# A fourth buffer for the low halves of the streamed weights, and two 16 KB pairs for the large activations

## The chip, the cores and the metric

The kernel runs on one core of a Trainium2 chip. The metric is the device time of one execution in microseconds (us); lower is better. The core's engines work side by side, each through its own list of instructions: TensorE (PE) multiplies, with its weight loads shown apart as PEld; VectorE (DVE) and ScalarE (ACT) do the elementwise work; GpSimd (POOL) does next to nothing here; SyncE (SP) issues the DMA transfers. Instructions wait for each other by semaphores.

## The reference

A sequence of 256 tokens of width 1024 goes through two blocks of two layers each, all in float32.

```python
# block 1, for l in range(2)
sh1, sc1, gt1, sh2, sc2, gt2 = split(silu(c) @ w_ada[l] + b_ada[l], 6)
u = x * (1 + sc1) + sh1
y = mixer(u, ...)          # proj = u @ w_in; attention (8 heads, rope) and a conformer conv, 31 taps
x = layer_norm(ALPHA * x + (1 + gt1) * y, ...)
u = x * (1 + sc2) + sh2
h = square(relu(u @ w_up[l])) @ w_down[l]
x = layer_norm(ALPHA * x + (1 + gt2) * h, ...)
# block 2, two layers: rmsnorm, a mixer of three attention branches (dilated windows, differential,
# latent) with a gate each, then rmsnorm and a gated feed-forward, hidden width 2816; last a final norm
```

## The kernel before, in words

**Exact products from two halves.** Every weight and every large activation is split into a high half (`hi`, rounded to the type that TensorE multiplies) and a low half (`lo`, the rest); a product is `hi*hi + hi*lo + lo*hi`. The weights come as tiles of 1 MB (128 partitions by 2048 numbers), one `fetch` (L124) each: SP issues the load into `raw` (L131), ACT makes `whi` (L138), DVE makes `wlo` (L139), each in two halves of 128x1024. The pools hold 3 `raw`, 4 `whi` and 3 `wlo`. `w` (L146) keeps up to two tiles ready ahead of the one in use.

**The products.** `ws2` (L166) multiplies a tile with an activation that lies feature-major (L175 the hi of the weight, eight matmuls of 512 columns; L177 its lo, eight of 256). `Out` (L236) adds a tile into the output accumulators (L206 to L208, 24 matmuls of a tile: hi by hi, hi by lo, lo by hi). It holds back the last two tiles of an output projection for `tail`. `as_512` (L211) is the first projection behind a norm: it takes two tiles at once, called C and D below, and runs them token half by token half (L222, L223, L228).

**The handover.** Between two stages the old output has to be finished, added to x and normed, and the next projection begun. `handover` (L663) does it by an order written out by hand for PE, DVE and ACT: tail of token half 0, norm of half 0 beside the tail of half 1, then the first projection of half 0 beside the norm of half 1. In block 1 the norm is a LayerNorm (L761 gate, L765 add, L768 moments, L304 the inverse root, L778 and L779 scale, L732 transposes on PE, L794 and L796 the affine part, L801 the hi of the new activation `u`, L803 its lo). In block 2 it is an RMSNorm (L841 add, L845, L828 squares, L880, L304, L883 scale, L732 transposes, L907 hi of `u`, L905 lo). The one from block 1 to block 2 does both (L870, L874, L877 between). There are eight handovers; seven of them begin a next stage with `as_512`.

**What sets the order.** PE's order is written by hand throughout. On DVE, ACT and SP a scheduler places the instructions outside the handovers, and puts those that belong to the fetches (`with self.later()`) where their tile buffers come free by its own reckoning; they may also fall into a handover's sequence. Within an engine, an instruction that waits holds up all that stand behind it. Side work (columns of the conditioning vector, L374; the bias tables) is dealt out between the matmuls by `tick`. In the feed-forward of layer 0 this includes a table that goes through DRAM: its transfer is issued at L613 (`toep`).

**The large activations.** `new_u` (L348) gives the normed activation, hi and lo in one 16 KB tile of the pool `u2`, which has one buffer. The mixers' gates `gt`, the merged result `mg`, the conv's `xT` and others come from `s8`, four tiles of 8 KB; block 2 has one more of 8 KB in `s8x`.

Of the kernel before, what the change touches and what calls it, by code (L numbers as in the profile page):

```python
# [9 lines left out]
F32 = mybir.dt.float32  # L10
F32R = mybir.dt.float32r
# [5 lines left out]
P = 128  # L17
D = 1024
S = 256
KT = D // P  # L20
# [44 lines left out]
class Net:  # L65
    def __init__(self, ctx, tc, ins, out, stop=None, dump=None):
        self.tc, self.nc, self.i, self.out = tc, tc.nc, ins, out
        self.stop, self.dumps = stop, dump or {}
        self.uid = 0
        self.pools = {}  # L70
        for name, bufs in (("raw", 3), ("whi", 4), ("wlo", 3), ("s8", 4), ("u2", 1), ("s4", 7), ("b4", 2), ("one", 1), ("sm", 3)):
            self.pool(ctx, name, bufs)
        self.pool(ctx, "ps", 8, space=PSUM)
        self.pool(ctx, "dr", 1, space=bass.MemoryType.DRAM)
        self.queue = weight_order(ins)
        self.ready = []
        self.tracks = []
        self.behind = []
        self.ada = {}

# [266 lines left out]

    def new_u(self):  # L348

        t = self.t("u2", [P, 2, KT, S], F32R)  # L350
        return t[:, 0], t[:, 1], t

    def new_fm(self, n=KT, pool="s8"):
        return self.t(pool, [P, n, S], F32R), self.t(pool, [P, n, S], F32R)

    def par_(self, name, at, n=1):
# [173 lines left out]
    def start(self):  # L530


        nc, i = self.nc, self.i
        self.c_row = self.t("G", [P, D], tag="c_row")
        c_row = self.row(i["c"])
        self.par = self.t("one", [P, NPC], tag="par")
        nc.sync.dma_start(self.par, i["params"])
        for lo, hi in HALVES:
            th = self.c_row[:, lo:hi]
            nc.scalar.activation(th, c_row[:, lo:hi], AF.Tanh, scale=0.5)  # L540
            nc.vector.scalar_tensor_tensor(th, th, 1.0, c_row[:, lo:hi], op0=ALU.add, op1=ALU.mult)
        a, n = PC["b_ada"]
        self.par1 = self.t("one", [P, n], tag="par1")
        nc.vector.tensor_scalar(self.par1, self.par[:, a:a + n], 1.0, None, op0=ALU.add)
        u = self.new_u()
        xT = self.t("s8", [P, KT, S])
        A, B = self.ada_cols(0, 1), self.ada_cols(0, 0)
        ps = [self.ps() for _ in range(8)]
        self.con = self.t("one", [P, NCC], tag="con")
        self.ident = self.con[:, 0:P]  # L550
        a, n = CC["cmask"]
        self.cmask = self.con[:, a:a + n]
        self.x = self.t("one", [P, 2, D], tag="x")
        for k in range(KT):
            wa = self.t("raw", [P, 2048])
            for lo, hi in ((0, 1024), (1024, 2048)) if k == 0 else ((0, 2048),):
                nc.sync.dma_start(wa[:, lo:hi], i["w_ada_0"][k, :, lo:hi])
            lo, hi = {0: (0, 1), 1: (1, 4), 4: (4, 8)}.get(k, (0, 0))
            if hi:
                nc.sync.dma_start(xT[:, lo:hi, :], i["xT"][:, lo:hi, :])  # L560
            if k == 0:
                self.fetch(2)
            self.ada_dot(0, 1, k, wa[:, 0:1024])
            self.ada_dot(0, 0, k, wa[:, 1024:2048])
            nc.vector.tensor_scalar(xT[:, k, :], xT[:, k, :], A[:, k:k + 1], B[:, k:k + 1], op0=ALU.mult, op1=ALU.add)
            self.split(u[0][:, k, :], u[1][:, k, :], xT[:, k, :])
            w = self.w(ahead=0)
            for g in range(3):
                for h in range(2):
                    self.as_(ps[2 * g + h], w, slice(512 * g, 512 * g + 512), u, k, h, k == 0, k == KT - 1)  # L570
            mm = nc.tensor.matmul
            for m in range(4):
                o = ps[6 + m // 2][:, (m % 2) * S:(m % 2) * S + S]
                b = slice((12 + m) * P, (13 + m) * P)
                grp = dict(skip_group_check=True)
                mm(o, w[0][:, b], u[0][:, k, :], start=k == 0 and m % 2 == 0, stop=False, **grp)
                mm(o, w[0][:, b], u[1][:, k, :], start=False, stop=False, **grp)
                mm(o, w[1][:, b], u[0][:, k, :], start=False, stop=k == KT - 1, **grp)
        self.ones = self.t("one", [P, P], tag="ones")
        nc.vector.memset(self.ones, 1.0)  # L580
        th = self.small(KT, "c_t")
        c = self.par_("c", 0, KT)
        nc.scalar.activation(th, c, AF.Tanh, scale=0.5)
        self.c_sel = self.t("one", [P, KT, 32], tag="c_sel")
        nc.vector.memset(self.c_sel, 0.0)
        self.c_col = self.t("one", [P, KT], tag="c_col")
        nc.vector.scalar_tensor_tensor(self.c_col, th, 1.0, c, op0=ALU.add, op1=ALU.mult)
        nc.vector.tensor_scalar(self.c_col, self.c_col, 0.5, None, op0=ALU.mult)
        nc.vector.tensor_copy(self.c_sel[:, :, 0:1], self.c_col[:, :, None])
        return u, ps  # L590
# [399 lines left out]
    def mixer1(self, l, u, ps):  # L990
# [58 lines left out]
        def qkf(h):  # L1049
            r = slice(64 * (h % 2), 64 * (h % 2) + 64)  # L1050
            return qT[r, h // 2, :], kT[r, h // 2, :]
        gt = [self.t("s8", [P, KT, S]) for _ in range(2)]

        def gates(b, cs):
            for c in cs:
# [38 lines left out]
        gates(1, [3])  # L1094
        self.finish(ada)
        self.dump(f"hc{l}", hc[0].bitcast(F32))
        mg = self.new_fm()

        def merge(s):
            nc.vector.tensor_add(gt[0][:, s, :], gt[0][:, s, :], gt[1][:, s, :])  # L1100
# [108 lines left out]
    def mixer2(self, l, u, ps):  # L1209
# [1 line left out]
        gq = self.row(i["mla_g"][l])  # L1211

        pcs = [[p for _, p in ps], [p for _, p in self.as_512(u)]]
        n_ = self.new_fm()
        mn = self.mla_norm(pcs, gq, n_)
        next(mn)
        wkr = self.w()
# [59 lines left out]
            kcs.append(kc)  # L1277
        next(gka)
        qTc = self.t("s8x", [P, 8, S])
        kTc = self.t("s8", [P, 8, S])  # L1280
        for src, dst in ((qcs, qTc), (kcs, kTc)):
            for h in range(2):
                tok = slice(h * P, (h + 1) * P)
# [37 lines left out]
            self.dump(f"yb{l}", y[0].bitcast(F32))  # L1321
        ab = self.track(rest(), 22, 62)

        gt = [self.t("s8x" if b == 1 else "s8", [P, KT, S]) for b in range(3)]
        bh = self.small(24, "bgh")
        nc.vector.tensor_scalar(bh, self.par_("b_gate", l * 24, 24), 0.5, None, op0=ALU.mult)
        for b in (2, 0, 1):
            for c in range(4):
                w = self.w()
                for m in range(2):  # L1330
# [2 lines left out]
                    nc.scalar.copy(g, p[:, S:])  # L1333
                    nc.vector.tensor_add(g, p[:, :S], g)
                    nc.scalar.activation(g, g, AF.Tanh, scale=0.5, bias=bh[:, b * 8 + k:b * 8 + k + 1])
        mg = self.new_fm()
        for b in (2, 0, 1):
            if b == 1:
                self.finish(ab)
# [123 lines left out]
def weight_order(i):  # L1463

    o = []
    for l in range(L):
        w = i["w_in_a" if l == 0 else "w_in_b"]
        o += [w[c] for c in range(w.shape[0])]
        last = o.pop()
        o += [i["w_attn_br"][l, c] for c in range(2)] + [last]  # L1470
        for name in ("w_conv_pw", "w_out"):
            o += [i[name][l, c] for c in range(i[name].shape[1])]
        o += [i["w_up"][l, c] for c in range(3)]
        for c in range(3, 19):
            if c < 16:
                o.append(i["w_up"][l, c])
            o.append(i["w_down"][l, c - 3])
    for l in range(L):
        w = i["w_in2"][l]
        o += [w[c] for c in range(4)] + [i["w_kr"][l]] + [w[c] for c in range(4, 7)]  # L1480
        o += [i["w_uq"][l, c] for c in range(3)] + [i["w_ukv"][l, 0]]
        o += [w[c] for c in range(7, 16)]
        for b in (2, 0, 1):
            o += [i["w_gate"][l, b * 4 + c] for c in range(4)]
        for b in "cab":
            o += [i[f"w_br_{b}"][l, c] for c in range(2)]
        o += [i["w_o"][l, c] for c in range(4)]
        o += [i["w_fgu"][l, c] for c in range(4)]
        for c in range(2, 13):
            if c < 11:  # L1490
                o += [i["w_fgu"][l, 2 * c], i["w_fgu"][l, 2 * c + 1]]
            o.append(i["w_fd"][l, c - 2])
    return o


def build(tc, ins, out, stop=None, dump=None):
    with ExitStack() as ctx:
        net = Net(ctx, tc, ins, out, stop, dump)
        ctx.enter_context(tc.manual_schedule(engines={mybir.EngineType.PE}))
        with ExitStack() as c1:  # L1500
            for name, bufs in (("ada", 2), ("G", 1)):
                net.pool(c1, name, bufs)
            net.block1()
        if stop is None or stop.startswith("2"):
            with ExitStack() as c2:
                for name, bufs in (("bias", 3), ("s8x", 1)):
                    net.pool(c2, name, bufs)
                net.block2()
        net.dump("x", net.x)
# [148 lines left out]
```

## Time and profile before

| | us |
|---|---|
| median of 3 runs | 1733.07 (1732.88 to 1734.87) |
| the profiled execution | 1733.14 |
| its span, first to last instruction | 1731.2 |
| PE busy | 1661.8 (96%) |
| DVE busy | 1281.8 (74%) |
| ACT busy | 958.8 (55%) |
| mean granted clock of TensorE, share of full speed | 0.989 |

The page of the profile gives the busy time of each engine, the chain of work that ended last, and the groups of instructions that cost most. Matmuls overlap, so PE's busy time is not its work at full speed. In the rows below a timeline line reads: start, duration, engine, line of the kernel, operation, what it writes and reads, its shape, how many in a row (x2 and so on are one piece), and in square brackets the idle time of the engine before it and what ended it.

### The profile page before, as it was taken

The numbers are of one execution on the slowest core, as the hardware profiler recorded it, in microseconds if no ns is written. First come the engines' busy times: TensorE is split into PE (matmuls) and PEld (weight loads), VectorE is DVE, ScalarE is ACT, GpSimd is POOL, SyncE is SP. The second block draws the span as 40 slices with busy tenths as digits, with TensorE's granted clock in tenths as the row PEclk, the third lists the DMA queues.
The fourth block names the chain that finished last, engine by engine and source line by source line (L and its number), as shares of the span: only waits on it lengthen the run. The fifth ranks groups of instructions, "written<-read, shape, count | busy, mean of one in ns | idle before, by whom it ended". The sixth has DMA issues, their size and how long they took to land.

```text
span 1731.2 us, 25828 instructions
## 1 busy us (share of the span) xinstructions
PE 1661.8 (96%) x10008; PEld 1436.9 (83%) x10008; DVE 1281.8 (74%) x2497; ACT 958.8 (55%) x1750; POOL 2.6 (0%) x12
## 2 busy tenths in 40 slices
PE   6998999998999999997999999999999999999998
PEld 5887888787888888885988898888889888988887
DVE  7999788578997886557856677766676566876665
ACT  3564375464355375553566754655455677455553
POOL 0000000000000000000000000000000000000000
PEclk9999999999999999998999999999999999999999
DMA  8884568584874466653544444555545444445551
GB/s 337 342 318 173 199 223 316 196 294 176 308 247 182 171 229 233 219 192 140 208 152 150 147 151 179 195 195 195 191 150 203 149 147 146 164 168 198 182 190 72
DMA packets 59974, 347.37 MB, mean 201 GB/s; under 512 B 6558, under 2 KB 10700, under 8 KB 25676
## 3 DMA queue, kind: packets, MB, share of 16 engines
q1 hardware_dynamic: 59852, 345.73, 55.3%
q8 instruction: 78, 1.28, 0.3%
q14 instruction: 44, 0.36, 0.1%
HBM read 344.63 MB, written 2.64 MB: 201 GB/s over the span
## 4 chain that ended last, share of the span: by engine, by line
PE 89%; DVE 7%; DMA 2%; ACT 1%; issue 0%; SPq 0%; DVEq 0%; ACTq 0%
PE ps L175 23%; PE ps L177 12%; PE ps L207 8%; PE ps L206 8%; PE ps L208 8%; PE ps L160 5%; PE ps L161 5%; PE ps L164 4%; PE ps L228 3%; PE ps L222 3%; PE ps L223 2%; DVE wlo L139 2%; PE ps L439 1%; PE ps L332 1%; PE ps L487 1%; PE ps L464 1%
## 5 line engine op out<-in xcount | busy, mean ns | idle before, releaser
L139 DVE TENSOR_TENSOR wlo<-raw,whi 128x1024 fp32r<-128x1024 f32 (+1 forms) x534 | 629.7, 1211 | 206.3 <-PE ps L177 104.0
L138 ACT CAST whi<-raw 128x1024 fp32r<-128x1024 f32 (+1 forms) x534 | 534.1, 1043 | 279.4 <-PE ps L208 80.6
L175 PE MATMUL ps<-u,whi 128*128 128x512 f32 x1728 | 438.9, 396 | 0.0
L175 PEld LDWEIGHTS ps<-u,whi 128*128 128x128 f32 x1728 | 313.9, 188 | 65.3 <-issue 5.7
L206 PE MATMUL ps<-whi,s 128*128 128x512 f32 (+2 forms) x688 | 253.6, 369 | 3.8 <-ACT whi L138 3.8
L207 PE MATMUL ps<-wlo,s 128*128 128x512 f32 (+2 forms) x688 | 253.0, 368 | 0.5 <-DVE wlo L139 0.5
L208 PE MATMUL ps<-whi,s 128*128 128x512 f32 (+2 forms) x688 | 252.3, 367 | 0.0
L177 PEld LDWEIGHTS ps<-u,wlo 128*128 128x128 f32 x1728 | 235.6, 190 | 17.2
L177 PE MATMUL ps<-u,wlo 128*128 128x256 f32 x1728 | 240.7, 282 | 0.0
L206 PEld LDWEIGHTS ps<-whi,s 128*128 128x128 f32 x688 | 130.3, 189 | 23.9 <-ACT whi L138 4.0
L208 PEld LDWEIGHTS ps<-whi,s 128*128 128x128 f32 x688 | 130.0, 189 | 21.0 <-DVE s L151 0.7
L207 PEld LDWEIGHTS ps<-wlo,s 128*128 128x128 f32 x688 | 130.2, 189 | 19.8 <-DVE wlo L139 1.2
L222 PE MATMUL ps<-whi,u 128*128 128x512 f32 x240 | 98.2, 409 | 11.0 <-ACT u L801 10.9
L188 ACT COPY ev<-ps 128x256 f32<-128x256 f32 x136 | 50.2, 369 | 92.1 <-PE ps L177 92.1
L952 DVE SCALAR_TENSOR_TENSOR s<-s,dw,s 128x255 f32<-128x255 f32 (+17 forms) x240 | 96.2, 462 | 0.0
L223 PE MATMUL ps<-wlo,u 128*128 128x512 f32 x240 | 96.0, 400 | 0.0
L160 PE MATMUL ps<-u,whi 128*128 128x256 f32 x352 | 89.4, 292 | 0.2 <-DVE s L941 0.2
L161 PE MATMUL ps<-u,whi 128*128 128x256 f32 x352 | 85.9, 282 | 0.0
L160 PE MATMUL ps<-s,whi 128*128 128x256 f32 x320 | 82.4, 289 | 0.0
L161 PE MATMUL ps<-s,whi 128*128 128x256 f32 x320 | 81.0, 285 | 0.3 <-DVE s L151 0.3
L189 DVE TENSOR_TENSOR ev<-ps,ev 128x256 f32<-128x256 f32 x136 | 56.8, 420 | 28.9 <-ACT ev L188 28.1
L151 DVE TENSOR_TENSOR s<-ev,s 128x256 fp32r<-128x256 f32 (+1 forms) x72 | 39.1, 542 | 48.9 <-PE ps L207 37.7
(263 smaller groups left out, 2123.2 us busy)
## 6 DMA issues: line engine op xcount, KB each, us to landing
raw<-in_w_fgu_dram SPq DMA_DIRECT2D x44, 1024.0 KB, 4.8
raw<-in_w_up_dram SPq DMA_DIRECT2D x32, 1024.0 KB, 5.0
raw<-in_w_down_dram SPq DMA_DIRECT2D x32, 1024.0 KB, 5.6
raw<-in_w_in_dram SPq DMA_DIRECT2D x32, 1024.0 KB, 4.8
ada<-in_w_ada_p_dram SPq DMA_DIRECT2D x48, 512.0 KB, 5.1
raw<-in_w_gate_dram SPq DMA_DIRECT2D x24, 1024.0 KB, 4.8
raw<-in_w_fd_dram SPq DMA_DIRECT2D x22, 1024.0 KB, 4.8
raw<-in_w_in_b_dram SPq DMA_DIRECT2D x18, 1024.0 KB, 6.1
```

The costliest lines, as they stand in the source:

```text
L138: nc.scalar.copy(hi[:, a:b], raw[:, a:b])
L139: nc.vector.tensor_sub(lo[:, a:b], raw[:, a:b], hi[:, a:b].bitcast(F32))
L160: mm(ps, whi[:, b], ahi[:, k, :], start=j == 0, stop=False)
L161: mm(ps, whi[:, b], alo[:, k, :], start=False, stop=False)
L175: mm(p2, whi[:, (blk + k) * P:(blk + k + 1) * P], both[:, :, k, :], start=k == 0, stop=False)
L177: mm(p[:, :S], wlo[:, (blk + k) * P:(blk + k + 1) * P], uhi[:, k, :], start=False, stop=k == KT - 1)
L206: mm(ps, ahi[:, k, tok], whi[:, cols], start=first, stop=False, **grp)
L207: mm(ps, ahi[:, k, tok], wlo[:, cols], start=False, stop=False, **grp)
L208: mm(ps, alo[:, k, tok], whi[:, cols], start=False, stop=last, **grp)
L222: mm(p, ahi[:, k, tok], whi[:, cols], start=k == 0, stop=False)
L223: mm(p, ahi[:, k, tok], wlo[:, cols], start=False, stop=False)
L952: nc.vector.scalar_tensor_tensor(cv[:, ct, d:], hp[:, ct, :S - d], wk, cv[:, ct, d:], op0=ALU.mult, op1=ALU.add)
```

## The change

The pool `wlo` gets a fourth buffer of 8 KB. To make room, the four 8 KB tiles of `s8` and the single 16 KB tile of `u2` become two 16 KB tiles, `ua` and `ub`; `new_u` gives them in turns, so that mixers have their `u` in `ua` and feed-forwards in `ub`; gates and other tiles that lived in `s8` take halves of the pair that is not in use (`gt`, `n_`, `xT` in `ub`, `mg` in `ua`, which the mixer's `u` has left by then). `s8x` gets a second buffer. No computation is added or removed.

```diff
-("raw", 3), ("whi", 4), ("wlo", 3), ("s8", 4), ("u2", 1), ("s4", 7), ...
+("raw", 3), ("whi", 4), ("wlo", 4), ("u2", 1), ("s4", 7), ...
+        self.turn = False
...
     def new_u(self):
-        t = self.t("u2", [P, 2, KT, S], F32R)
+        self.turn = not self.turn
+        t = self.pair("ua" if self.turn else "ub", F32R)
         return t[:, 0], t[:, 1], t
-    def new_fm(self, n=KT, pool="s8"):
+    def pair(self, tag, dt=F32):
+        return self.t("u2", [P, 2, KT, S], dt, tag=tag)
+    def new_fm(self, n, pool):
...
-        xT = self.t("s8", [P, KT, S])
+        xT = self.pair("ub")[:, 0]
...
-        gt = [self.t("s8", [P, KT, S]) for _ in range(2)]
+        gt = self.pair("ub")
+        gt = [gt[:, b] for b in range(2)]
...
-        mg = self.new_fm()
+        mg = self.pair("ua", F32R)
+        mg = mg[:, 0], mg[:, 1]
...
-        n_ = self.new_fm()
+        n_ = self.pair("ub", F32R)
+        n_ = n_[:, 0], n_[:, 1]
...
-        kTc = self.t("s8", [P, 8, S])
+        kTc = self.t("s8x", [P, 8, S])
...
-        gt = [self.t("s8x" if b == 1 else "s8", [P, KT, S]) for b in range(3)]
+        gt = self.pair("ub")
+        gt = [gt[:, 0], self.t("s8x", [P, KT, S]), gt[:, 1]]
...
-                for name, bufs in (("bias", 3), ("s8x", 1)):
+                for name, bufs in (("bias", 3), ("s8x", 2)):
```

PE's order is the same before and after. The same instructions stand on DVE, ACT and SP, in another order at some places. Lines move by one up to `new_u`, and by six to ten behind it: L139 (`wlo`) becomes L140, L138 (`whi`) L139, L150 and L151 become L151 and L152, L419 and L421 become L425 and L427, L374 becomes L380, L761 and L794 become L767 and L800, L841 and L905 become L847 and L911.

First, DVE in a LayerNorm handover (from the feed-forward of layer 0 to the mixer of layer 1). Before, `wlo_3757` is the lo of tile C and `wlo_3765` that of tile D; these stand ahead of the handover and within it:

```order
L139 TENSOR_TENSOR wlo_3725<-raw_3722,whi_3724 128x1024 x2
L139 TENSOR_TENSOR wlo_3757<-raw_3754,whi_3756 128x1024 x2
L761 TENSOR_TENSOR ev_3819<-ps_2559,G_497_3192 128x512
...
L761 TENSOR_TENSOR ev_3901<-ps_2561,G_497_3192 128x512
L765 SCALAR_TENSOR_TENSOR x_119<-x_119,ev_3901 128x512
L768 BN_STATS bn_604_3900<-x_119 128x6
L139 TENSOR_TENSOR wlo_3765<-raw_3762,whi_3764 128x1024 x2
L794 TENSOR_SCALAR ev_3898<-ps_3876,pl_a_3775,pl_b_3776 128x128 x2
```

Now, with C as `wlo_3752` and D as `wlo_3760`:

```order
L140 TENSOR_TENSOR wlo_3752<-raw_3749,whi_3751 128x1024 x2
L140 TENSOR_TENSOR wlo_3760<-raw_3757,whi_3759 128x1024 x2
L767 TENSOR_TENSOR ev_3814<-ps_2554,G_495_3187 128x512
...
L767 TENSOR_TENSOR ev_3896<-ps_2556,G_495_3187 128x512
L771 SCALAR_TENSOR_TENSOR x_116<-x_116,ev_3896 128x512
L774 BN_STATS bn_602_3895<-x_116 128x6
L800 TENSOR_SCALAR ev_3893<-ps_3871,pl_a_3770,pl_b_3771 128x128 x2
```

The two instructions for D's lo moved from just before the affine part to ahead of the handover. The other six handovers that begin with `as_512` differ in the same way.

Second, DVE in an RMSNorm handover (the first within block 2). Before:

```order
L883 TENSOR_SCALAR s_1666_10398<-s_1666_10398,r_r_10443 128x512
L841 SCALAR_TENSOR_TENSOR x_119<-ps_10274,x_119 128x512
L139 TENSOR_TENSOR wlo_10351<-raw_10348,whi_10350 128x1024 x2
L905 TENSOR_TENSOR u_1664_10358<-ps_10453,u_1664_10358 128x2x128
L905 TENSOR_TENSOR u_1664_10358<-ps_10454,u_1664_10358 128x2x128
L841 SCALAR_TENSOR_TENSOR x_119<-ps_10275,x_119 128x256 x2
```

Now, where `wlo_10341` is D's lo:

```order
L140 TENSOR_TENSOR wlo_10333<-raw_10330,whi_10332 128x1024 x2
L140 TENSOR_TENSOR wlo_10341<-raw_10338,whi_10340 128x1024 x2
L847 SCALAR_TENSOR_TENSOR x_116<-ps_10262,x_116 128x512
...
L889 TENSOR_SCALAR s_1659_10388<-s_1659_10388,r_r_10433 128x512
L847 SCALAR_TENSOR_TENSOR x_116<-ps_10264,x_116 128x512
L911 TENSOR_TENSOR ub_10348<-ps_10443,ub_10348 128x2x128
L911 TENSOR_TENSOR ub_10348<-ps_10444,ub_10348 128x2x128
L847 SCALAR_TENSOR_TENSOR x_116<-ps_10265,x_116 128x256 x2
```

Here too D's lo left the sequence between the add of half 1 and the lo of `u`.

Third, ACT in the feed-forward of layer 0. Before, `whi_3229` is a tile of `w_down` that the next output addition needs, and `whi_3268` and `whi_3329` are the two behind it; `s_517` is an activation:

```order
L188 COPY ev_3274<-ps_3302 128x256
L1118 ACTIVATE ev_3274<-ev_3274 128x512
L1119 ACTIVATE ev_3274<-ev_3274 128x512
L150 CAST s_517_3323<-ev_3274 128x512
L138 CAST whi_3229<-raw_3227 128x1024 x2
L138 CAST whi_3268<-raw_3266 128x1024 x2
L138 CAST whi_3329<-raw_3327 128x1024 x2
L188 COPY ev_3374<-ps_3375 128x256
```

Now, with the same three tiles as `whi_3224`, `whi_3263` and `whi_3324`:

```order
L151 CAST s_484_3122<-ev_3078 128x512
L139 CAST whi_3224<-raw_3222 128x1024 x2
L189 COPY ev_3169<-ps_3170 128x256
...
L1127 ACTIVATE ev_3269<-ev_3269 128x512
L151 CAST s_515_3318<-ev_3269 128x512
L139 CAST whi_3263<-raw_3261 128x1024 x2
L139 CAST whi_3324<-raw_3322 128x1024 x2
L189 COPY ev_3369<-ps_3370 128x256
```

The cast of the `w_down` tile moved two feed-forward steps ahead; the other two stay behind the activation's cast. On SP the load of that tile now stands ahead of the transfer of `toep` instead of behind it. On DVE the lo of the second tile (`wlo_3264`) now stands behind four instructions that wait for that output addition or for what follows it:

```order
L152 TENSOR_TENSOR s_516_3319<-ev_3269,s_515_3318 128x512
L425 TENSOR_TENSOR G_495_3187<-ps_3354,b_445_2876 128x256
L427 TENSOR_SCALAR G_495_3187<-G_495_3187 128x256
L380 ISA ada_3258,ada_513_3293<-ada_3258,c_row_92,par_95 128x1024
L380 ISA ada_513_3293 128x1
L140 TENSOR_TENSOR wlo_3264<-raw_3261,whi_3263 128x1024 x2
```

Before, both halves of this lo stood ahead of that L152 (then L151) and of L419 and L421 (now L425 and L427).

## Rows read from the trace of the kernel before

**Rows 1.** The page: PE's busy time, and the chain's shares by engine.
```profile
PE 1661.8 (96%) x10008; PEld 1436.9 (83%) x10008; DVE 1281.8 (74%) x2497; ACT 958.8 (55%) x1750; POOL 2.6 (0%) x12
...
PE 89%; DVE 7%; DMA 2%; ACT 1%; issue 0%; SPq 0%; DVEq 0%; ACTq 0%
```

**Rows 2.** PE's waits: line, waited for: us in total, times, longest.
```profile
PE ps L732 <- DVE s L883: 18.0, 8, 8.3
...
PE ps L222 <- ACT u L801: 10.9, 6, 3.0
PE ps L967 <- DVE s L952: 5.8, 1, 5.8
```

**Rows 3.** The chain that ended last, longest pieces: start, us, what.
```profile
210.64 2.36 DVE wlo L139 x2
...
1535.76 2.36 DVE wlo L139 x2
```

**Rows 4.** Timeline of DVE, second LayerNorm handover.
```profile
397.42 0.69 DVE L761 TENSOR_TENSOR ev<-ps,G 128x512 f32<-128x512 f32 x1 [0.53 <-PE ps L208]
...
400.29 0.42 DVE L761 TENSOR_TENSOR ev<-ps,G 128x256 f32<-128x256 f32 x1 [0.67 <-PE ps L208]
...
407.27 2.36 DVE L139 TENSOR_TENSOR wlo<-raw,whi 128x1024 fp32r<-128x1024 f32 x2
409.55 0.72 DVE L794 TENSOR_SCALAR ev<-ps,pl_a,pl_b 128x128 f32<-128x128 f32 x2
```

**Rows 5.** Timeline of ACT, the same handover.
```profile
394.70 2.01 ACT L138 CAST whi<-raw 128x1024 fp32r<-128x1024 f32 x2 [3.43 <-PE ps L208]
...
406.63 0.81 ACT L796 ACTIVATE ev<-ps,pl_b,pl_a 128x128 f32<-128x128 f32 x2 [0.86 <-PE ps L732]
```

**Rows 6.** Timeline of PE, the same handover.
```profile
411.03 0.50 PE L222 MATMUL ps<-whi,u 128*128 128x512 f32 x1 [3.02 <-ACT u L801]
```

**Rows 7.** Timeline of DVE, handover from block 1 to block 2.
```profile
783.44 2.35 DVE L139 TENSOR_TENSOR wlo<-raw,whi 128x1024 fp32r<-128x1024 f32 x2
785.71 0.21 DVE L304 TENSOR_SCALAR r_w<-r_t 128x1 f32<-128x1 f32 x1
```

**Rows 8.** Timeline of PE, the same handover.
```profile
792.43 1.94 PE L732 MATMUL ps<-con,s 128*128 128x128 f32 x8 [8.28 <-DVE s L883]
```

**Rows 9.** Timeline of DVE, first RMSNorm handover.
```profile
1067.05 0.42 DVE L841 SCALAR_TENSOR_TENSOR x<-ps,x 128x256 f32<-128x256 f32 x1 [1.46 <-PE ps L208]
...
1073.23 2.36 DVE L139 TENSOR_TENSOR wlo<-raw,whi 128x1024 fp32r<-128x1024 f32 x2 [1.25 <-PE ps L207]
```

**Rows 10.** Timeline of PE, the same handover.
```profile
1080.79 1.06 PE L732 MATMUL ps<-con,s 128*128 128x128 f32 x8 [1.75 <-DVE s L883]
```

**Rows 11.** Timeline of PE, feed-forward of layer 0, an output addition.
```profile
336.18 0.80 PE L206 MATMUL ps<-whi,s 128*128 128x512 f32 x1 [3.84 <-ACT whi L138]
...
341.54 0.39 PE L208 MATMUL ps<-whi,s 128*128 128x512 f32 x1
...
344.27 0.39 PE L208 MATMUL ps<-whi,s 128*128 128x512 f32 x1
...
344.74 2.19 PE L175 MATMUL ps<-u,whi 128*128 128x512 f32 x8
```

**Rows 12.** Timeline of ACT, the same stretch.
```profile
335.08 5.78 ACT L138 CAST whi<-raw 128x1024 fp32r<-128x1024 f32 x6
```

**Rows 13.** Timeline of DVE, the same stretch.
```profile
338.43 1.28 DVE L374 CUSTOM_DVE_ANT_0 ada<-ada,c_row,par 128x1024 f32<-128x1024 f32 x1
...
344.47 0.69 DVE L151 TENSOR_TENSOR s<-ev,s 128x512 fp32r<-128x512 f32 x1 [1.27 <-PE ps L207]
...
345.79 2.35 DVE L139 TENSOR_TENSOR wlo<-raw,whi 128x1024 fp32r<-128x1024 f32 x2
```

**Rows 14.** Stretches behind the first two LayerNorm handovers: us, busy PE PEld DVE ACT POOL, PEclk, DMA, GB/s.
```profile
216.00:222.00 6.00, 6.00 (x27) 4.97 (x26) 4.27 (x16) 1.48 (x3) 0.00 (x0) 0.81 0.19 78
...
412.00:418.00 6.00, 5.52 (x29) 4.34 (x28) 5.18 (x17) 2.38 (x6) 0.00 (x0) 1.00 0.30 126
```

## What the change will do to the time: the prediction

> **What bounds the kernel now.** I read the page first: PE is busy for 1661.8 of 1731.2 us, and the chain that ended last is 89% PE and 7% DVE [rows 1]. So the time is PE's stream plus the places where PE stands still, and a gain must come from those. PE's list of waits names them: 18.0 us for the scaled rows of the RMS-type norms (8 times), 10.9 us for the first `u` behind the LayerNorms (6 times), and one wait of 5.8 us at the end of the first conv [rows 2]. The chain then shows what is on the path in these places. Seven pieces of two `wlo` halves stand in it within a handover, each 2.36 or 2.35 us, from 210.64 to 1535.76 [rows 3]. The timelines of three handovers and of one odd stretch in the first feed-forward, read in that order, give the terms.
>
> PE's order is not changed, so every PE instruction can only start earlier or later by what releases it. I go through the places where a releaser moves.
>
> **LayerNorm handovers (three).** In the second one D's lo starts on DVE at 407.27, and the affine part L794 behind it at 409.55: 2.28 us in which DVE does nothing for this handover [rows 4]. L794 need not wait for anything else there: ACT's first affine piece, from the same transposes, already started at 406.63 [rows 5]. PE starts the new projection at 411.03, after 3.02 us of idling for ACT's `u`, 1.48 us after L794 started [rows 6]. With D's lo gone from this place L794 starts at about 407.27 and PE at 408.75; it was free at 411.03 - 3.02 = 408.01, so 0.74 us of the wait stays and 2.28 goes. D's lo now stands ahead of the handover. Its hi was cast by 394.70 + 2.01 = 396.71 [rows 5], its second half takes 1.2 us, so it is done near 398.0, 0.6 us after the first gate (L761) began before at 397.42. The next but two gate waits 0.67 us for PE anyway [rows 4]; that hides the delay, and if the cover were gone it would cost 0.6. The first and third LayerNorm handovers hold the same piece, and among the six waits of [rows 2] the longest is 3.0: I take 3 x 2.28 = **6.8 us**. Ends: 3 x (2.28 - 0.6) = 5.0 and 3 x 2.36 = 7.1.
>
> **From block 1 to block 2.** D's lo stands in the chain of the inverse root: it starts at 783.44, the next step of the root at 785.71 [rows 7]. PE waits for this chain for 8.28 us, until 792.43 [rows 8], so DVE alone sets the end and the pitch of 2.27 comes back nearly whole; the root's step before it overlaps a little, and I take **2.2**. Ends: 1.6 (with 0.6 for a late start) and 2.3.
>
> **RMSNorm handovers within block 2 (three).** Here D's lo sits at 1073.23, after DVE has itself waited 1.25 us for a `wlo` buffer that PE's tail (L207) frees [rows 9]. Without it the second half of the norm could come some 1.25 + 2.28 = 3.5 us earlier for DVE's part. But PE waits only 1.75 us for it [rows 10]; past that PE's own matmuls are the limit. So 1.75 each, **5.2 us**. The earlier place may start the handover's first add late; the add at 1067.05 follows an idle of 1.46 us [rows 9], which hides 0.6. Ends: 3 x 1.1 = 3.3 (0.6 not hidden) and 3 x 2.05 = 6.2 (if the small gap ahead of L228, some 0.3, goes too).
>
> [...]
>
> **The stretch in the first feed-forward.** At 336.18 PE starts an output addition after waiting 3.84 us for a hi cast [rows 11]; ACT casts three tiles in one run from 335.08 [rows 12], because all three stand behind an activation's cast (the order's third place). Now the first of them is cast two steps earlier, and its load stands ahead of the table's transfer. So the addition can start when PE is free, at 336.18 - 3.84 = 332.34. At full clock its 24 matmuls take 24 x 0.2275 = 5.46 us (twelve from 341.54 to 344.27), and with the 0.24 us up to 344.74 the next tile starts at 332.34 + 5.46 + 0.24 = 338.04 instead of 344.74 [rows 11]: 6.70 us earlier. Something is late next: that tile's lo. It now stands behind L152, L425, L427 and L380. L152 starts, as before, 0.2 us after the last matmul of the addition (344.27 and 344.47), that is at 337.77; from it to the lo's start there were 1.32 us (344.47 to 345.79), and the L380 adds 1.28 [rows 13]: the lo starts at 340.37 and its first half is there at about 341.5. PE reaches its use after eight matmuls, at 338.04 + 1.82 = 339.86. So PE waits about 1.65 us again, and I take 6.70 - 1.65 = **5.0 us**. Ends: 0, if the cast waits for its load as before, and 6.7, if no new stall comes.
>
> **The clock.** After the first LayerNorm's stall the granted clock is 0.81 in six us in which PE is fully busy, after the second it is 1.00 in the corresponding six [rows 14]. That is 6.00 x 0.19 = 1.1 us which a shorter stall may give back. I take half, **0.5**. Ends: -0.5 and 1.1. [...]
>
> **The rest of the change at nothing.** The pairs are coarser tiles than the 8 KB ones, so a writer of one half could wait for a reader of the other. In the listed orders I find no instruction of the critical stretches that moved because of it. In block 2 outside the handovers PE waits little, and DVE is free for a quarter of the time [rows 1]. If that cover is gone, a late `gt` or `mg` would cost PE directly, up to a few us per layer; I take 0, with ends of -1 and +1. In the first mixer six lo halves stand 1 to 10 us of DVE work earlier; their matmuls are not the ones that PE waits for, so 0 too, and the rival below for the rest.
>
> **Sum.** 6.8 + 2.2 + 5.2 + 5.0 + 0.5 = 19.7 us off the profiled execution's 1733.14, which lies 0.07 from the median of 1733.07: **1713.4 us**. The sums of the ends of the main terms (without a missing stretch) give 1709 to 1717 for this case alone.
>
> **Rivals.**
> 1. The stretch gives nothing: the `w_down` cast, now early in ACT's list, waits for its load, or the new stall at the lo is as long as the old one. For it: the lo now stands behind four instructions, and before PE was at low speed there, so the full-speed end is an estimate. Against: the load is issued earlier now. 1713.4 + 5.0 = 1718.4.
> 2. The handovers give half: D's lo waits for its buffer or its hi ahead of the first add, and all of the norm starts late. For it: row 1073.23's 1.25 us [rows 9]. Against: a fourth buffer is what it waited for. Half of 14.2 is 7.1: 1720.5.
> 3. More than the sum: no new stall in the stretch, and the gaps ahead of L228 go: 1713.4 - 1.7 - 0.9 = 1710.8.
> 4. The change does not do what it says: the order moves but the time of D's lo is bound elsewhere (raw tiles, of which there are still three): 1733.
> 5. Slower, in the first mixer. DVE sets the end of the conv there, and PE already waits 5.8 us for it [rows 2]. Six lo halves now stand earlier in DVE's list. If each waits for its load and cast, DVE stands still and the conv's end moves by the same. With the longest wait of that stage, 5.8, for each: 34.8 us lost against 19.7, 1748.2. It decides from 3.9 us per half (23.2 us, the gain and 0.2%). Against it: a hi cast was nowhere waited for by PE for more than 3.84 [rows 11], and the halves move by less than a tile's work.
>
> **Chances.** The sum 0.62; rival 1 0.17; rival 2 0.09; rival 3 0.05; rival 4 0.03; rival 5 0.04. The range holds 0.8 with 1709 to 1720: the sum's own range, rivals 1 and 3, and the near part of rival 2. About 0.2% (3.5 us) is what a measurement of this kernel can tell from no change. Faster by more than that: 0.62 + 0.17 + 0.09 + 0.05 = 0.93; within it 0.03; slower 0.04.
>
> **What would show it.** Right: no `wlo` piece in the chain within the seven handovers; PE's wait for L801's successor at 0.7 us instead of 3.02; the wait of 8.28 near 6.1; the three waits of 1.75 gone; the output addition near 332 without a wait and a new wait for a `wlo` of 1 to 2 us some eight us later. Wrong: D's lo ahead of the handover with an idle of more than 1 us in front of it, a longer wait than 5.8 at the first conv's end, a wait for a hi cast or a load in the stretch near 332, or waits of PE for `gt` or `mg` which the trace before does not have.

## The result and the profile after

The changed kernel takes 1710.46 us (median, 1709.15 to 1711.35) against 1732.97 us of the kernel before, run beside it: a ratio of 0.9868 with a 95% interval of 0.9851 to 0.9885, 22.5 us less. The forecast was 1713.4 with a range of 1709 to 1720. The profiled execution took 1711.08 us, with a span of 1709.3.

The page of the changed kernel answers to [rows 1]:

```profile
PE 1656.0 (97%) x10008; PEld 1433.8 (84%) x10008; DVE 1276.3 (75%) x2497; ACT 956.6 (56%) x1750; POOL 2.6 (0%) x12
...
PE 88%; DVE 8%; DMA 1%; ACT 1%; issue 1%; SPq 0%; ACTq 0%; DVEq 0%
```

The span fell by 21.9 us, PE's busy time by 5.8. So 16.1 us of the gain are idle time of PE, and the rest is the same matmuls taking less time, which fits the mean granted clock (0.989 before, 0.992 now). PE's list of waits (line, waited for: us in total, times, longest) answers to [rows 2]:

```profile
PE ps L738 <- DVE s L889: 11.8, 5, 6.1
...
PE ps L973 <- DVE s L958: 5.8, 1, 5.8
PE ps L738 <- DVE x L784: 4.7, 6, 1.1
...
PE ps L223 <- ACT ub L807: 2.3, 4, 0.6
...
PE ps L178 <- DVE wlo L140: 1.3, 1, 1.3
PE ps L223 <- ACT ua L807: 1.2, 2, 0.6
```

Two of the three named waits shrank, and one is new. The RMS-type wait went from 18.0 to 11.8 us and from eight places to five; the one for `u` from 10.9 to 3.5 (2.3 and 1.2, its tile has two names now); the conv's 5.8 stayed. The 1.3 for a `wlo` at L178 was not in the list before.

Since PE's order is the same, the two traces can be laid side by side at PE's transposes (L732, now L738), of which each handover has two groups. The time between two such points, before and after:

| stretch | before | after | gain | forecast |
|---|---|---|---|---|
| start to the first handover | 208.89 | 209.33 | -0.44 | 0 |
| first LayerNorm handover | 11.78 | 8.37 | 3.41 | 2.28 + 0.5 |
| feed-forward of layer 0, with the odd stretch | 184.85 | 179.70 | 5.15 | 5.0 |
| second LayerNorm handover | 10.82 | 8.37 | 2.45 | 2.28 |
| mixer of layer 1 | 180.16 | 178.82 | 1.34 | 0 |
| third LayerNorm handover | 10.82 | 8.37 | 2.45 | 2.28 |
| feed-forward of layer 1 and the norm into block 2 | 185.11 | 182.96 | 2.15 | 2.2 |
| the rest of the handover into block 2, and the first mixer of block 2 | 279.10 | 279.93 | -0.83 | 0 |
| three RMSNorm handovers | 9.26 each | 7.18 each | 6.3 | 5.2 |

The gains sum to 22.0, and the two profiled executions differ by 1733.14 - 1711.08 = 22.1.

### The profile page after: what moved, and what is told of

Its sections match the earlier page's. It is cut to its first block, busy times and chain, and to the rows that moved or that the text cites. A ratio compares the mean times of both kernels' runs of the same rounds, so it can differ in the third digit from the quotient of the medians.

```text
span 1709.3 us, 25828 instructions
## 1 busy us (share of the span) xinstructions
PE 1656.0 (97%) x10008; PEld 1433.8 (84%) x10008; DVE 1276.3 (75%) x2497; ACT 956.6 (56%) x1750; POOL 2.6 (0%) x12
## 4 chain that ended last, share of the span: by engine, by line
PE 88%; DVE 8%; DMA 1%; ACT 1%; issue 1%; SPq 0%; ACTq 0%; DVEq 0%
PE ps L176 23%; PE ps L178 12%; PE ps L207 7%; PE ps L208 7%; PE ps L209 7%; PE ps L161 5%; PE ps L162 5%; PE ps L165 5%; PE ps L223 3%; PE ps L229 3%; PE ps L224 3%; DVE wlo L140 1%; PE ps L445 1%; PE ps L333 1%; DMA raw<-in_w_in_a_dram 1%; PE ps L493 1%
## 5 line engine op out<-in xcount | busy, mean ns | idle before, releaser
L140 DVE TENSOR_TENSOR wlo<-raw,whi 128x1024 fp32r<-128x1024 f32 (+1 forms) x534 | 631.8, 1212 | 258.0 <-ACT whi L139 255.3
L139 ACT CAST whi<-raw 128x1024 fp32r<-128x1024 f32 (+1 forms) x534 | 535.0, 1043 | 279.7 <-PE ps L209 72.8
L176 PE MATMUL ps<-ub,whi 128*128 128x512 f32 x1088 | 273.2, 393 | 0.0
L176 PEld LDWEIGHTS ps<-ub,whi 128*128 128x128 f32 x1088 | 198.6, 188 | 37.5
L207 PE MATMUL ps<-whi,s 128*128 128x512 f32 (+1 forms) x464 | 174.6, 376 | 0.0
L208 PE MATMUL ps<-wlo,s 128*128 128x512 f32 (+1 forms) x464 | 174.3, 376 | 0.0
L209 PE MATMUL ps<-whi,s 128*128 128x512 f32 (+1 forms) x464 | 173.9, 375 | 0.0
L176 PE MATMUL ps<-ua,whi 128*128 128x512 f32 x640 | 165.7, 401 | 0.0
L178 PEld LDWEIGHTS ps<-ub,wlo 128*128 128x128 f32 x1088 | 148.3, 190 | 12.4 <-DVE wlo L140 1.8
L178 PE MATMUL ps<-ub,wlo 128*128 128x256 f32 x1088 | 151.8, 282 | 1.3 <-DVE wlo L140 1.3
L176 PEld LDWEIGHTS ps<-ua,whi 128*128 128x128 f32 x640 | 115.3, 188 | 27.8 <-issue 5.7
L958 DVE SCALAR_TENSOR_TENSOR s<-s,dw,s 128x255 f32<-128x255 f32 (+14 forms) x240 | 96.3, 462 | 0.0
L178 PEld LDWEIGHTS ps<-ua,wlo 128*128 128x128 f32 x640 | 87.2, 190 | 6.5
L161 PE MATMUL ps<-ua,whi 128*128 128x256 f32 x352 | 89.3, 292 | 0.3 <-DVE s L947 0.3
L178 PE MATMUL ps<-ua,wlo 128*128 128x256 f32 x640 | 89.1, 282 | 0.0
L162 PE MATMUL ps<-ua,whi 128*128 128x256 f32 x352 | 85.9, 282 | 0.0
```

Of the source, the lines that this page charges most:

```text
L139: nc.scalar.copy(hi[:, a:b], raw[:, a:b])
L140: nc.vector.tensor_sub(lo[:, a:b], raw[:, a:b], hi[:, a:b].bitcast(F32))
L161: mm(ps, whi[:, b], ahi[:, k, :], start=j == 0, stop=False)
L162: mm(ps, whi[:, b], alo[:, k, :], start=False, stop=False)
L176: mm(p2, whi[:, (blk + k) * P:(blk + k + 1) * P], both[:, :, k, :], start=k == 0, stop=False)
L178: mm(p[:, :S], wlo[:, (blk + k) * P:(blk + k + 1) * P], uhi[:, k, :], start=False, stop=k == KT - 1)
```

## Inside the stretches

DVE in the second LayerNorm handover (start, us, ..., idle before and what ended it), to be read beside [rows 4]. First two lines of before that are not there, C's lo and the moments:

```profile
394.53 2.36 DVE L139 TENSOR_TENSOR wlo<-raw,whi 128x1024 fp32r<-128x1024 f32 x2 [2.48 <-issue]
...
406.73 0.43 DVE L768 BATCH_NORM_STATS2 bn<-x 128x6 f32<-128x256 f32 x1
```

And now:

```profile
387.66 2.36 DVE L140 TENSOR_TENSOR wlo<-raw,whi 128x1024 fp32r<-128x1024 f32 x2 [3.08 <-ACT whi L139]
389.93 0.68 DVE L767 TENSOR_TENSOR ev<-ps,G 128x512 f32<-128x512 f32 x1
...
392.16 0.42 DVE L767 TENSOR_TENSOR ev<-ps,G 128x256 f32<-128x256 f32 x1
...
398.61 0.43 DVE L774 BATCH_NORM_STATS2 bn<-x 128x6 f32<-128x256 f32 x1
398.96 0.71 DVE L800 TENSOR_SCALAR ev<-ps,pl_a,pl_b 128x128 f32<-128x128 f32 x2
```

PE in the same place, beside [rows 6]:

```profile
400.43 0.50 PE L223 MATMUL ps<-whi,ua 128*128 128x512 f32 x1 [0.53 <-ACT ua L807]
```

The affine part (L800) follows the moments at once, where D's lo stood before, and PE waits 0.53 us instead of 3.02. D's lo now waits for its hi ahead of the handover, and the first gate (L767) starts in the same instant as it ends. That gate stands 7.47 us ahead of the first transposes (397.40), where it stood 8.10 us ahead of them before (405.52): 0.6 us late, as the prediction reckoned. The gate at 392.16, which waited 0.67 us for PE before, now shows no idle time. The late start has eaten that cover whole, and no more: the first transposes wait 1.10 us, as before (1.09). Nothing is left to spare. In the first and the third LayerNorm handover the chain that ended last now runs through D's lo ahead of the first gate, though no longer through a lo inside the handover (start, us, what):

```profile
199.64 2.36 DVE wlo L140 x2
...
574.90 2.36 DVE wlo L140 x2
```

The prediction had named an idle of more than 1 us in front of D's lo as a sign that it is wrong. That idle is there, 3.08 us in this handover and as long in the first RMSNorm one below, and PE shows no loss by it. The sign was badly chosen: before, DVE idled about as long in this place (2.48 us ahead of C's lo, 0.53 ahead of the gate), and what counts is how late the gate starts.

The first gate stood on DVE behind a lo that waited 3.08 us for its hi, and started 2.27 us after that lo did (387.66 and 389.93). What that costs depends on the cover; here it cost PE nothing that the trace shows.

DVE in the first RMSNorm handover, beside [rows 9]:

```profile
1046.90 2.36 DVE L140 TENSOR_TENSOR wlo<-raw,whi 128x1024 fp32r<-128x1024 f32 x2 [3.08 <-ACT whi L139]
1049.17 0.68 DVE L847 SCALAR_TENSOR_TENSOR x<-ps,x 128x512 f32<-128x512 f32 x1
...
1057.74 0.76 DVE L911 TENSOR_TENSOR ub<-ps,ub 128x256 fp32r<-128x256 f32 x2 [1.44 <-ACT ub L913]
```

And PE there, beside [rows 10]:

```profile
1063.03 1.06 PE L738 MATMUL ps<-con,s 128*128 128x128 f32 x8
```

The wait of 1.75 us is gone from the view. DVE even idles 1.44 us for ACT's hi of `u` now: with D's lo away, PE is the limit from one group of transposes to the next.

PE in the feed-forward of layer 0, beside [rows 11]:

```profile
329.27 0.40 PE L207 MATMUL ps<-whi,s 128*128 128x512 f32 x1
...
334.98 2.19 PE L176 MATMUL ps<-ub,whi 128*128 128x512 f32 x8
338.52 1.22 PE L178 MATMUL ps<-ub,wlo 128*128 128x256 f32 x8 [1.34 <-DVE wlo L140]
```

DVE there, beside [rows 13]:

```profile
334.77 0.69 DVE L152 TENSOR_TENSOR s<-ev,s 128x512 fp32r<-128x512 f32 x1 [4.47 <-PE ps L208]
...
336.04 1.28 DVE L380 CUSTOM_DVE_ANT_0 ada<-ada,c_row,par 128x1024 f32<-128x1024 f32 x1
...
337.24 2.35 DVE L140 TENSOR_TENSOR wlo<-raw,whi 128x1024 fp32r<-128x1024 f32 x2
```

The output addition starts without a wait, the next tile 5.71 us behind it (8.56 before), and then PE waits 1.34 us for the lo that stands behind L152, the gate's add and L380, as the prediction had it (1.65). The other 2.85 us went because PE ran this addition at full clock (1.00 from 329.2 to 334.9, against 0.50 from 336.0 to 340.0 before; its first matmul takes 0.40 us, 0.80 before) and no longer waits 0.47 us for a lo within it.

The granted clock behind the first two LayerNorm stalls, beside [rows 14] (us, busy PE PEld DVE ACT POOL, PEclk, DMA, GB/s). PEclk is the mean granted clock of a stretch, as a share of full speed: behind the first stall of before, the stretches of half a us show 0.50 each from 215.0 to 218.0 and 1.00 each from 218.5 to 220.0, and the six us from 214 together show 0.72. Now:

```profile
214.00:220.00 6.00, 5.18 (x27) 3.80 (x25) 4.53 (x16) 2.35 (x5) 0.00 (x0) 1.00 0.00 0
402.00:408.00 6.00, 5.29 (x27) 3.88 (x25) 4.60 (x16) 2.34 (x5) 0.00 (x0) 1.00 0.00 0
```

No fall behind a wait of 0.5 us; that is the 1.0 us which the first handover gained beyond the others.

## The experiments

**Theory A**: the fourth `wlo` buffer does it all, by taking D's lo out of the handovers and by the early cast; a handover gains only what PE waited for. The rivals stand in the expectations.

**The pairs alone.** The changed kernel with three `wlo` buffers.

```diff
-("whi", 4), ("wlo", 4), ("u2", 1)
+("whi", 4), ("wlo", 3), ("u2", 1)
```

> The two pairs and their turns alone, wlo with three buffers as before; every engine's order is then that of the kernel before. Theory A (the gain is D's lo out of the handovers and the early cast, both by the fourth wlo buffer): no change, 1733 us within 1.5, and D's lo again in the chain of the seven handovers. Rival P (the turns of the pairs themselves let norms or gates start earlier): at least a quarter of the 22.5 us, 1727 or less. Rival C (a 16 KB tile makes writers of one half wait for readers of the other, a cost that the fourth buffer outweighs): 1735 or more.

Measured: 1734.27 against 1735.05 us, ratio 0.9992 (0.9981 to 1.0002). PE waits for the RMS-type norms at eight places again, 8.3 us at the longest:

```profile
PE ps L738 <- DVE s L889: 19.4, 8, 8.3
```

So neither the turns nor the larger tiles cost or give anything that can be measured. The changed kernel differs from this one in that one count, so its whole gain comes with the fourth buffer. The fourth buffer with the old pools was not tried.

**D's lo back in its place.** `fetch` keeps D's lo back, and the handover issues it where it stood (two of the three kinds of handover are shown).

```diff
+                if hold:
+                    self.held.append((lo, raw, hi, a, b))
+                else:
                     nc.vector.tensor_sub(lo[:, a:b], raw[:, a:b], hi[:, a:b].bitcast(F32))
...
             steps(3)
+            net.put_held()
             for k in range(4):
                 affine(k)
...
             next(fill, None)
+            net.put_held()
             sub(0)
```

> The changed kernel with the two instructions of D's lo put back into all seven handovers, at the places of the kernel before (in the one from block 1 to block 2 a few short instructions earlier); four wlo buffers and the pairs stay, nothing else moves but one load on SP. Theory A, from the rows: each of the three LayerNorm handovers costs 2.3 to 2.5 again, the first one 1.0 more by its clock, the one into block 2 2.2, and the three RMSNorm ones only 0.5 to 0.8 each, since D's lo no longer waits 1.25 us for its buffer in there: 12 us together, 1722.5. Rival B (the place is all, the buffer wait nothing): 16 us, 1726.5. Rival N (only the buffer matters, the place doesn't): 1710.5.

Measured: 1724.23 us, ratio to the kernel before 0.9942 (0.9930 to 0.9955); 14.1 more than the changed kernel's 1710.15 in the run further below. PE in the second LayerNorm and the first RMSNorm handover, and the clock behind the first LayerNorm one:

```profile
408.20 0.50 PE L233 MATMUL ps<-whi,ua 128*128 128x512 f32 x1 [2.82 <-ACT ua L820]
...
1078.30 1.06 PE L750 MATMUL ps<-con,s 128*128 128x128 f32 x8 [0.85 <-DVE s L902]
```

```profile
217.00:223.00 6.00, 6.00 (x19) 4.72 (x20) 5.33 (x17) 2.72 (x6) 0.00 (x0) 0.72 0.41 162
```

DVE in that RMSNorm handover: D's lo stands inside again, and no wait for a buffer stands ahead of it.

```profile
1070.75 2.35 DVE L129 TENSOR_TENSOR wlo<-raw,whi 128x1024 fp32r<-128x1024 f32 x2
```

Between the transposes the three LayerNorm handovers take 11.6 us each (8.37), the norm into block 2 waits 8.28 (6.13), and the RMSNorm ones take 7.92 (7.18). That is 9.7 + 2.15 + 2.2 = 14.1, as between the medians. (The profiled execution itself took 1728.12 us, 17.0 more than the profiled one of the changed kernel in that run; 2.1 of the other 2.9 lie ahead of the first handover.) The RMSNorm ones cost 0.74, not 2.1: the rest of their gain went with the 1.25 us wait for a buffer. Theory A was right in the stalls and too low in the sum, since the clock fell behind all three LayerNorm stalls (0.72 in the six us behind each) and not only the first. Rival N falls by the time, and rival B by the 0.74 us, where it had 2.1.

**The early cast alone, in the kernel before.** In the feed-forward of layer 0 the second copy of an up product must stand behind the next tile's hi and lo (`issue_after` sets that order). The loads keep their order on SP.

```diff
+            with ExitStack() as st:
+                if self.first and m >= 1:
+                    for i in self.made[len(self.made) - len(self.ready):][:1]:
+                        st.enter_context(self.tc.issue_after(i[0].ins))
+                        st.enter_context(self.tc.issue_after(i[1].ins))
-            self.nc.scalar.copy(tm, p[:, S:])
-            self.nc.vector.tensor_add(tm, p[:, :S], tm)
+                self.nc.scalar.copy(tm, p[:, S:])
+                self.nc.vector.tensor_add(tm, p[:, :S], tm)
```

> The kernel before, three wlo buffers and the old pools; only in the feed-forward of layer 0 the next tile's hi and lo must stand ahead of the second copy of an up product, which moves one w_down cast from behind the activation's cast to ahead of that copy and leaves the rest. Theory A (the 3.84 us stall there and the half clock behind it come from the cast's place in ACT's list; its load had long landed): the stall goes and, as the lo behind it is not moved back, no new one comes: 6 to 7 us, 1726.5. Rival D (the cast waits for its load behind the table's transfer): no change, 1733.

Measured: 1728.88 against 1735.05 us, ratio 0.9957 (0.9944 to 0.9971), 6.2 us. PE and ACT in the stretch:

```profile
332.01 0.40 PE L214 MATMUL ps<-whi,s 128*128 128x512 f32 x1
...
337.76 2.19 PE L178 MATMUL ps<-u,whi 128*128 128x512 f32 x8
```

```profile
329.25 2.01 ACT L140 CAST whi<-raw 128x1024 fp32r<-128x1024 f32 x2
```

The cast ran at 329.25, so its load had landed; no wait is left in the stretch, and the tile behind starts 5.75 us after the addition. From the last transposes of the first handover to the first of the second this kernel takes 6.8 us less than the profiled kernel before. So the stall came from the order of instructions on ACT, and no fourth buffer is needed to remove it.

**The new wait removed, in the changed kernel.** Two edges of order put the lo ahead of the activation's lo and of the gate's add (`lo_first(n)` places what stands in it behind the lo of the next n tiles).

```diff
+        with self.lo_first(1):
-        nc.vector.tensor_add(g, p[:, :256], bb[:, n * 256:(n + 1) * 256])
+            nc.vector.tensor_add(g, p[:, :256], bb[:, n * 256:(n + 1) * 256])
...
-            self.split(hs[0], hs[1], t.rearrange("p (m t) -> p m t", m=2))
+            with self.lo_first(2):
+                self.split(hs[0], hs[1], t.rearrange("p (m t) -> p m t", m=2))
```

> The changed kernel; in the feed-forward of layer 0 the lo of the next up tile must stand ahead of the activation's lo and of the gate's add, which moves one pair of lo halves ahead of three DVE instructions that wait for the output addition. Theory A: the new wait of 1.34 us goes, 1.3 us faster, 1709.2. Rival: the lo is late for another reason (its hi or its load), no change.

Measured: 1708.55 us (1708.45 to 1708.97). DVE and PE there:

```profile
332.36 2.36 DVE L142 TENSOR_TENSOR wlo<-raw,whi 128x1024 fp32r<-128x1024 f32 x2 [1.77 <-ACT whi L141]
```

```profile
334.07 2.19 PE L179 MATMUL ps<-ub,whi 128*128 128x512 f32 x8
336.11 1.11 PE L181 MATMUL ps<-ub,wlo 128*128 128x256 f32 x8
```

The wait of 1.34 is gone. The changed kernel and this version, side by side on one chip:

> The changed kernel, beside e10 on one chip and for comparison with it: 1710.3 us, as in its two runs so far.

> The version of e4 beside the changed kernel on one chip. Theory A: 1.3 us faster than e9, 1709. Rival: the 1.9 us between e4 and the first runs of the changed kernel were chance, the same time as e9.

Measured: 1710.40 (1709.72 to 1712.42) and 1708.31 us (1708.02 to 1709.28). The runs of the two do not overlap: this version beats both kernels, by 2.1 us the changed one. In the profiles 1.6 us of that lie in the feed-forward itself (179.7 us from the first handover to the second in e9, 178.1 in e10); the rest is not traced to the edit. Its ratio to the kernel before is 0.9849 (0.9833 to 0.9864).

**Half of the lo in the handover.**

```diff
-                if hold:
+                if hold and a:
                     self.held.append((lo, raw, hi, a, b))
```

> The changed kernel with only the second half of D's lo (1.14 us of DVE) put back into the seven handovers, the first half stays ahead. Theory A (a handover pays only for what the engine that ends last waits): the LayerNorm ones pay 1.14 each, the one into block 2 1.14, the RMSNorm ones nothing, since DVE has room there until PE is through; 4.6 us over the changed kernel, 1715, and no fall of the clock behind stalls of 1.7 us. Rival L (a handover pays in proportion to the DVE work in it): half of what the whole lo cost, 6.8 us, 1717.3.

Measured: 1714.82 us, ratio 0.9880 (0.9860 to 0.9900), 4.7 over the changed kernel. PE in the first LayerNorm and the first RMSNorm handover, and the clock:

```profile
214.68 0.50 PE L233 MATMUL ps<-whi,ub 128*128 128x512 f32 x1 [1.66 <-ACT ub L820]
...
1067.62 1.06 PE L750 MATMUL ps<-con,s 128*128 128x128 f32 x8
```

```profile
214.50:219.50 5.00, 4.82 (x20) 3.68 (x20) 4.61 (x17) 2.25 (x7) 0.00 (x0) 1.00 0.49 197
```

A first LayerNorm handover of 9.46 us (8.37, so 1.09 for 1.14 us of work), a wait of 7.14 into block 2 (6.13), and RMSNorm handovers of 7.17, as without it. Theory A holds; the cost is not in proportion to DVE's work, and rival L's 1717.3 lies above every run.

**Both kernels again.**

> The kernel before once more, for its clock behind the three LayerNorm stalls of 3.02 us, and for its two waits on conditioning loads in the mixer of layer 1. Theory A: the stalls and places are the same, whether the clock falls behind a stall differs from run to run. Rival: the clock falls behind the first of the three only, each time; the two waits on loads come again.

> The changed kernel once more, for comparison with the others on this chip: 1710.5 us; no fall of the clock in the LayerNorm handovers, no wait on conditioning loads in the mixer of layer 1.

Measured: 1736.78 us in the one run of before, 1710.15 (1708.83 to 1711.57) of the changed kernel. The clock of before behind its three LayerNorm stalls:

```profile
214.00:220.00 6.00, 5.58 (x17) 4.47 (x18) 5.61 (x18) 3.21 (x7) 0.00 (x0) 0.72 0.54 175
411.00:417.00 6.00, 5.42 (x13) 4.27 (x14) 5.61 (x19) 3.24 (x7) 0.00 (x0) 0.50 0.48 175
603.00:609.00 6.00, 5.45 (x17) 4.34 (x18) 5.61 (x19) 3.23 (x7) 0.00 (x0) 0.72 0.54 175
```

Its handovers take 11.80, 12.84 and 11.83 us, where the first profile had 11.78, 10.82 and 10.82, with the same stalls. So the clock behind a stall of 3 us fell or not from run to run, and a fall cost 1.0 us where the six us had 0.72, 2.0 where they had 0.50. Of the waits on conditioning loads in the mixer of layer 1 (1.1 us in the first profile) 0.2 were left:

```profile
PE ps L439 <- DMA ada<-in_w_ada_p_dram: 0.2, 1, 0.2
```

The rival falls in both its parts. But these waits may be more than chance: the four profiles with three `wlo` buffers have 1.1, 0.2, 0 (e1) and 1.8 us of them (e3), the eight with four buffers none. Whether the fourth buffer takes them away, by when the loads are issued, no run shows.

**A version that gains nothing.** In the first mixer of the version of e4, PE gets the first half of the attention branch's projection ahead of the conv's transposes.

```diff
+        if first:
+            branch(0, y, 0, None)
         self.finish(conv)
...
         next(cl)
-        branch(0, y, 0, None)
-        next(cl)
+        if not first:
+            branch(0, y, 0, None)
+            next(cl)
         branch(0, y, 1, None)
+        if first:
+            next(cl)
```

> A version that may beat both: the changed kernel with the lo order of e4, and in the first mixer the first half of the attention branch's projection put ahead of the conv's transposes, so that PE has work while DVE ends the conv. Theory A: of the 5.8 us of waiting there, and the half clock behind it (about 1 us), 3 to 6 us go, and some return as a wait for the conv's norm: 1704 to 1706. Rival: the conv's norm ends that much later and the next projection waits as long, 1708.5.

Measured: 1710.61 us (1708.74 to 1711.84), no gain on 1708.3. PE's waits from 140 to 176 us:

```profile
PE ps L984 <- DVE s L969: 2.0, 1, 2.0
PE ps L427 <- ACT ev L452: 1.9, 1, 1.9
PE ps L165 <- DVE s L155: 1.4, 2, 1.0
PE ps L164 <- ACT s L154: 0.8, 1, 0.8
```

The 5.8 became 2.0, and 4.1 came back behind it, where the conv's norm and the casts are late. The rival was right that the wait only moves; its 1708.5 was 2.1 too low.

## Why the prediction was right, step by step

- **LayerNorm handovers.** Forecast 6.8, measured 2.45 twice and 3.41 with the clock. Right in the mechanism; the 0.17 us beyond 2.28 is the gap between the moments and what follows them (0.54 us before, 0.35 now). The late start was hidden by the cover named, and fills it (that gate is the next one behind the first, not the next but two).
- **Into block 2.** 2.2 forecast, 2.15 measured. But the row behind it is -0.83, which no step had: the clock behind the second stall of that handover was 0.50 in four us, where before it was 0.67. This too differs between runs: the same row is 280.4 in e6, the kernel before, and 279.1 in e9, the changed one.
- **RMSNorm handovers.** Forecast 1.75 each, measured 2.1, the upper end: the small gap ahead of L228 went too. e2 and e5 show the two parts, the buffer wait and the lo's own time.
- **The odd stretch.** 5.0 forecast, 5.15 measured, with a new wait of 1.34 for 1.65. e3 shows the cause, e4 the new wait's.
- **The clock.** This term was too small: 0.5 forecast, 1.0 in the profiled pair, and more elsewhere: with the same stalls, the three LayerNorm handovers together were 0.96 us above 3 x 10.82 in the first profile, 2.0 in e1, 2.8 in e3 and 4.0 in e6. In three of these profiles the six us behind a stall show a fall seven times of nine: in the first profile 0.72 behind the first stall and 1.00 behind the other two, in e3 0.72 behind all three, in e6 0.72, 0.50 and 0.72.
- **What was costed at nothing.** The pairs: nothing (e1). The first mixer: -0.44, no trace of the slower rival; the conv's 5.8 did not move. The mixer of layer 1 gave 1.34 that no step had; in e6 the kernel before itself took 1.0 less there. Chance or the fourth buffer, the runs leave it open; for the prediction it is luck.

In the profiled pair the gain was 22.0 for 19.7. Beyond the forecast were the mixer of layer 1 (1.34), the RMSNorm gap (1.1) and the first LayerNorm handover (0.6); the other LayerNorm handovers and the odd stretch add 0.5, and the rows of -0.44 and -0.83 take 1.3 back. The other 0.6 of the 2.9 us lie between the profiled execution and the median. That the median fell close to rival 3's 1710.8 proves nothing for that rival: the gaps ahead of L228 went, but the new stall, which it had left out, came. The terms' own ends were not added up quite right either: the five of them give about 1710 to 1719, not 1709 to 1717.

The median of the kernel before was 1732.97 beside the changed one and 1735 to 1736 in the later runs. In e6, 3.6 us above the first profile, the LayerNorm handovers with their clock took 3.0 us more (36.5 for 33.4); for the other runs the reason is not shown.

## What to carry to other kernels

A further buffer paid here because a producer's instruction, held up or put back by the old count, stood in the list of an engine that a chain waits for (2.45 us of each of two LayerNorm handovers went with it); look for such strangers in the lists of the handovers, not only for waits on the buffer. Price the move by the wait of the engine that ends last, and look for the cover of the place it moves to: half a lo was free in the RMSNorm handovers (7.17 us for 7.18) and cost nearly its whole length in the first LayerNorm one (1.09 of 1.14 us). And when one stall goes, read what now stands ahead of the next operand: two edges of order gave 2 us more.

## What the runs showed of the hardware

Behind the same stall of 3.02 us TensorE's granted clock stayed at 1.00, or fell so that six us showed 0.72 or 0.50, and this changed between runs of one kernel and between places in one run. Behind the stalls of e2, 2.82 us in the second handover, it fell three times of three (0.72 each), behind the 1.66 to 1.68 us of e5 never (1.00 each). The times spread less without these stalls: 1708.8 to 1712.4 us in twelve runs of the changed kernel and 1708.0 to 1709.3 in nine of the version of e4, against 1731 to 1741 of the kernel before in many more. That the clock is the reason is not shown: e3, with all three stalls, spread over 2.9 us in five runs.
